# A feed-forward layer in blocks on one core: a written order of products over two pairs, a tile of its own for the first product, and later loads of residual rows

## The chip, the core and the metric

The kernel runs on one core of a Trainium2 chip. The metric is the device time of one execution in microseconds; lower is better. A core has engines with an instruction stream each: PE (matmuls), DVE (elementwise work and multiply-adds), ACT (activations, copies, casts), POOL (here a few copies, and DMA issues) and SP (DMA issues). Streams run in their own order and wait for one another through semaphores. Sums of matmuls stand in PSUM banks (here 128 x 512), everything else in SBUF tiles.

## The reference

One decoder layer over 1024 positions and a width of 1024. Ahead of what matters here lie a norm, an input projection, a convolution branch and a state-space branch, gates and a second norm. Then comes the part in which the change stands:

```python
def conv_ffn(h, w_up, dw_w, dw_b, w_down):
    u = causal_dwconv(h @ w_up, dw_w, dw_b)        # w_up 1024 x 5632, 3 taps
    gate, val = jnp.split(u, 2, axis=-1)           # 2816 columns each
    return (jax.nn.silu(gate) * val) @ w_down      # 2816 x 1024

h = layer_norm(DN_ALPHA * h + conv_ffn(h), ln2_g, ln2_b)
```

All is float32.

## The kernel before

A float32 matmul is made of three: each operand is split into a rounded part and the rest (a cast on ACT, then a subtraction on DVE), and PE adds hi x hi, hi x lo and lo x hi (lines 166 to 168). The weights so split have two halves, w[:, 0] and w[:, 1].

**up.** The 5632 columns of w_up are 44 blocks of 128, taken as 22 pairs j; a pair has a gate block (ug) and a value block (uv), each 128 channels by 1024 positions, in an early and a late half of 512. Both blocks of a pair and both halves of positions come from seven products in place of eight, of four chunks of 128 in the inner dimension and three matmuls each, so 12 matmuls by 512 columns. The sums of the hidden rows which they need (b11, b21, b22, t1, t2, t3, t4) are made once ahead of it, those of the weights for each pair by up_weights: four additions on DVE over the loaded blocks ra and rb, and casts and subtractions into w_ue (for b11 and b21), w_s24 (for t2 and b22), w_s10 (t1 and t4) and w_s3 (t3).

For the first LEAD = 8 pairs the products b11 and b21 are made in advance (up_first) and lie in DRAM as first_scr; here these are called the lead pairs, with five products each (60 matmuls) in the main loop. The other 14 have all seven (84).

In up_rest, ps is a bank that holds b11; ACT copies it to s; PE adds t2 to the same bank, ACT copies that to s again; then t1 is added and copied to uv's late half, then b22 and copied to ug's late half. Each of these four steps waits for the copy of the one ahead of it, since PE goes on adding in the bank that ACT reads. The other bank, pz, holds t3 and then t3 + t4; DVE subtracts from both. py holds b21, which DVE adds to s for ug's early half. For a lead pair b11 is not computed: both halves of first_scr[j] are loaded into ug, and ACT copies the late half of it into ps (line 878) before PE adds to it. There are three u tiles; a pair takes two, in turn.

Behind the products, each block has a causal convolution with three taps (one step on ACT, line 894, and two on DVE, line 898), then silu on ACT, the product with the gate on DVE (line 909), and a store to DRAM (b11_scr, b2_scr) for down; every second pair combines its block with that of an earlier pair in four additions and stores t32_scr and t41_scr.

**down.** Seven products again, now each over 11 steps k of 12 matmuls; load(p, k) brings an activation block (dr from b11_scr, b2_scr, t32_scr or t41_scr) and weight blocks of w_down (c, do), casts and subtracts them into w_dn. load_rows brings the rows of the residual stream from DRAM into the tile rows, four halves of rows a call, on POOL's queue. Its calls stand at k == 4 of products 0, 1, 2 and 4.

**Order.** A scheduler orders each engine's instructions from the program's order and priorities: a block under tc.high_priority moves ahead by the number given. Pools with a number of buffers per tag hold back the writer of a tile until the last reader of its slot is done; the w tiles (tag w) have few slots, s has two, raw (rb) three. The helper that does the cast is split_pair (lines 740 and 741); product makes the matmuls; bank(i) takes a PSUM bank from one of two sets, shown as acc and sm.

Of the kernel before, what the change touches and what calls it, by code (L numbers as in the profile page):

```python
# [8 lines left out]
F32 = mybir.dt.float32  # L9
F32R = mybir.dt.float32r  # L10
AF = mybir.ActivationFunctionType
ALU = mybir.AluOpType
# [4 lines left out]
P = 128  # L17
D = 1024
T = 1024
# [37 lines left out]
def kernel(  # L57
# [35 lines left out]
    ident = const.tile([P, P], F32, name="ident")  # L93
    make_identity(nc, ident)
    state_stack = ExitStack()
    statep = state_stack.enter_context(pool("states", side="right"))
# [5 lines left out]
    V.memset(ones, 1.0)  # L102
    mean_w = const.tile([P, P], F32, name="mean_w")
    V.memset(mean_w, 1.0 / D)
    eps = const.tile([P, 1], F32, name="eps")
# [17 lines left out]
    V.tensor_scalar_mul(kind_neg, kind[:, 0:2], -1.0)  # L123
    pc = const.tile([P, PC_N + 80], F32, name="pc")
    a_log = statep.tile([P, HEADS], F32, name="a_log")
# [108 lines left out]
    def ln_in(hh):  # L234
        hT = big_tile(f"hT{hh}")
        with pool(f"lnin{hh}", side="right") as pl:
# [12 lines left out]
            if first:  # L249
                SY.dma_start(pc[:, :PC_N], pcol)  # L250
                SY.dma_start(a_log, prow[RW_AL : RW_AL + HEADS].partition_broadcast(P))
                SY.dma_start(dskip, prow[RW_SD : RW_SD + HEADS].partition_broadcast(P))
# [562 lines left out]
    def up_first(upp, fp, bl, j):  # L815

        if j < LEAD - 1:
            t = weights(wup[2 * j], f"ue{j}")
            w = [t[:, i, :] for i in range(2)]
        else:  # L820
            with tc.high_priority(offset=4000):
                st = wst.tile([P, D], F32, tag="st", name=f"st_ue{j}")
                SY.dma_start(st, wup[2 * j])
                w = [upp.tile([P, D], F32R, tag="o", bufs=3, name=f"ue{i}_{j}") for i in range(2)]
                A.copy(w[0], st)
                V.tensor_tensor(out=w[1], in0=st, in1=w[0].bitcast(F32), op=ALU.subtract)
        ps = bank(1)
        for q, block in enumerate(("b11", "b21")):
            product(ps, lambda i: w[i][:, q * HALF : (q + 1) * HALF], bl[block], q == 0)
            f = fp.tile([P, HALF], F32, tag="first", bufs=2, name=f"first{q}_{j}")  # L830
            A.copy(f, ps)
            A.dma_start(first_scr[j][1 - q], f)

# [22 lines left out]

    def up_rest(upp, us, bl, j, before, ws):

# [3 lines left out]
        ug, uv = us[2 * j % 3], us[(2 * j + 1) % 3]  # L862
        s = upp.tile([P, HALF], F32, tag="s", bufs=2, name=f"s{j}")
        early, late = slice(2, 2 + HALF), slice(2 + HALF, 2 + T)
        ps, pz = bank(1), bank(0)
        if ue:
            product(ps, lambda i: ue[:, i, :HALF], bl["b11"], True)
            A.copy(s, ps)
            py = bank(1)
            product(py, lambda i: ue[:, i, HALF:], bl["b21"], True)  # L870
            V.tensor_tensor(out=ug[:, early], in0=s, in1=py, op=ALU.add)
        else:
            with tc.high_priority(offset=2500):
                SY.dma_start(
                    ug[:, 2 : 2 + T].rearrange("p (q n) -> p q n", q=2),
                    first_scr[j].rearrange("q p n -> p q n"),
                )
            A.copy(ps, ug[:, late])
        product(ps, lambda i: w24[:, i, :HALF], bl["t2"], False)
        A.copy(s, ps)  # L880
        product(pz, lambda i: w3[:, i], bl["t3"], True)
        product(ps, lambda i: w10[:, i, :HALF], bl["t1"], False)
        A.copy(uv[:, late], ps)
        V.tensor_tensor(out=uv[:, late], in0=pz, in1=uv[:, late], op=ALU.subtract)
        product(pz, lambda i: w10[:, i, HALF:], bl["t4"], False)
        V.tensor_tensor(out=uv[:, early], in0=pz, in1=s, op=ALU.subtract)
        product(ps, lambda i: w24[:, i, HALF:], bl["b22"], False)
        A.copy(ug[:, late], ps)
        os = []
# [28 lines left out]
        if j < NK:  # L918
            G.dma_start(b11_scr[j], ov[:, early])
            return ov  # L920
        SY.dma_start(b2_scr[j - NK], ov)
        a, b, t = before, ov, og
        V.tensor_tensor(out=t[:, early], in0=a[:, late], in1=b[:, late], op=ALU.subtract)
# [6 lines left out]
    def down(upp, dp):  # L930
# [18 lines left out]

        def load_rows(p):  # L950
            t0, cs = {0: (0, E), 1: (0, L), 2: (4, L), 4: (4, E)}[p]
            for t in range(t0, t0 + 4):
                G.dma_start(rs[t][:, cs], h1_scr[t * P : (t + 1) * P, cs])
# [137 lines left out]
        for p, (banks, first, then) in enumerate(products):  # L1091
            end = NK - LAST if p == 6 else NK
            for k in range(end):
# [3 lines left out]
                if k == 4 and p in (0, 1, 2, 4):  # L1097
                    load_rows(p)
            ws = {k: load(p, k) for k in range(end, NK)}
# [24 lines left out]
    state_stack.close()  # L1124
    mixT = combine(1, hT, yT)
    ffn_stack = ExitStack()
    qp = ffn_stack.enter_context(pool("ffq", side="right"))
# [6 lines left out]
    with pool("firsts", side="right") as fp:  # L1134
        for j in range(LEAD):
            if j == LEAD - 1:
                ws = up_weights(upp, 0)
            up_first(upp, fp, bl, j)
    before = None
    for j in range(NF):  # L1140
        before, ws = up_rest(upp, us, bl, j, before, ws), None
    ffn_stack.close()
# [101 lines left out]
```

## Time and profile before

| | us |
|---|---|
| median of three runs | 2029.7 |
| lowest and highest | 2026.96, 2030.37 |
| the profiled execution | 2030.47 |
| its span in the trace | 2028.8 |
| PE busy in the span | 1975.8 (97%) |
| DVE busy | 1695.8 (84%) |
| ACT busy | 1017.4 (50%) |
| POOL busy | 175.5 (9%) |

In the profile L166 is a line of the kernel; a row of a group has the line, the engine, the operation, the tile written and the tiles read, the count, then busy time, mean ns of one, and the idle time of the engine ahead of them with what ended it. A row of the waits has who waits for whom, the total in us, the number of times and the longest. In rows in order of time the first two numbers are start and length. The mean granted clock of PE is 0.995 of full speed. up's main loop runs from about 1391 to 1800, and down from there to the end.

### The profile page before, as it was taken

How to read it: one execution, taken by the hardware profiler on the slowest of the kernel's cores; microseconds unless marked ns; L12 is line 12 of the kernel's file. 1: busy time of each engine (PE TensorE's matmuls, PEld its weight loads, DVE VectorE, ACT ScalarE, POOL GpSimd, SP SyncE). 2: the span in 40 equal slices, each digit the busy share in tenths (PEclk: the TensorE clock that was granted, in tenths of full speed). 3: DMA queues.
4: the chain of work that ended last, by engine and by line, in shares of the span. 5: the costliest groups of instructions: out<-in, count | busy, mean ns of one | idle time of the engine just before them, and what ended most of it. 6: DMA issues, size and time to landing. Idle time of an engine off the chain costs nothing.

```text
span 2028.8 us, 24542 instructions
## 1 busy us (share of the span) xinstructions
PE 1975.8 (97%) x9164; PEld 1622.4 (80%) x9164; DVE 1695.8 (84%) x2261; ACT 1017.4 (50%) x1480; POOL 175.5 (9%) x140
## 2 busy tenths in 40 slices
PE   7999999999999999999999999999999999999998
PEld 6888888888788888888888888887777777777886
DVE  7599999989766869999998976596897777788768
ACT  4465654556453356665454645364554534443432
POOL 2010101001400000110100130010000000030000
PEclk9999999999999999999999999999999999999999
DMA  6222233333546522222323354565342222367563
GB/s 219 94 64 93 79 103 104 99 104 101 175 131 220 194 94 73 91 81 77 126 89 104 109 167 139 186 234 202 135 172 83 99 107 102 101 252 252 176 225 109
DMA packets 96903, 272.20 MB, mean 134 GB/s; under 512 B 11088, under 2 KB 11088, under 8 KB 96784
## 3 DMA queue, kind: packets, MB, share of 16 engines
q1 hardware_dynamic: 88864, 246.78, 36.8%
q0 software_dynamic: 5616, 19.66, 2.5%
q10 hardware_dynamic: 2304, 4.20, 0.6%
q8 instruction: 72, 1.18, 0.2%
q14 instruction: 47, 0.39, 0.1%
HBM read 221.05 MB, written 49.55 MB: 133 GB/s over the span
## 4 chain that ended last, share of the span: by engine, by line
PE 72%; DVE 19%; DMA 4%; issue 3%; ACT 2%; SPq 0%; DVEq 0%; ACTq 0%
PE acc L166 19%; PE acc L167 19%; PE acc L168 19%; DVE c L420 6%; PE sm L168 3%; PE sm L166 3%; PE sm L167 3%; PE sm L534 2%; PE acc L357 1%; DVE xbc L375 1%; DVE fo L898 1%; DMA dr<-b_scr 1%; PE sm L515 1%; PE sm L192 1%; PE sm L523 1%
## 5 line engine op out<-in xcount | busy, mean ns | idle before, releaser
L420 DVE SCALAR_TENSOR_TENSOR c<-v,pc,c 128x512 f32<-128x512 f32 x480 | 374.9, 804 | 6.3 <-ACT c L409 4.9
L478 POOL TENSOR_TENSOR au<-seg_mv,head_of 128x1024 fp32r<-128x1024 f32 x32 | 76.4, 2388 | 959.1 <-PE sm L487 728.8
L166 PE MATMUL acc<-hT,w_c 128*128 128x512 f32 x352 | 141.0, 401 | 0.0
L167 PE MATMUL acc<-hT,w_c 128*128 128x512 f32 x352 | 140.6, 399 | 0.0
L168 PE MATMUL acc<-hT,w_c 128*128 128x512 f32 x352 | 138.4, 393 | 0.0
L898 DVE SCALAR_TENSOR_TENSOR fo<-u,pc,fo 128x1024 f32<-128x1024 f32 x88 | 111.4, 1279 | 7.5 <-ACT fo L894 7.4
L375 DVE SCALAR_TENSOR_TENSOR xbc<-u,pc,xbc 128x512 f32<-128x512 f32 x144 | 109.9, 775 | 0.7 <-ACT xbc L373 0.5
L166 PE MATMUL acc<-h1s,w_s 128*128 128x512 f32 x264 | 103.6, 396 | 6.3 <-ACT s L880 3.7
L167 PE MATMUL acc<-h1s,w_s 128*128 128x512 f32 x264 | 102.9, 390 | 0.0
L168 PE MATMUL acc<-h1s,w_s 128*128 128x512 f32 x264 | 102.8, 391 | 0.0
L167 PE MATMUL acc<-w_z,hT 128*128 128x512 f32 x256 | 100.8, 394 | 0.0
L166 PE MATMUL acc<-w_z,hT 128*128 128x512 f32 x256 | 100.8, 401 | 0.0
L168 PE MATMUL acc<-w_z,hT 128*128 128x512 f32 x256 | 100.7, 396 | 0.0
L1032 ACT CAST w_dn<-dr 128x1024 fp32r<-128x1024 f32 (+1 forms) x73 | 60.9, 842 | 75.8 <-DVE dr L962 37.8
L154 ACT CAST w_c<-st_c 128x1024 fp32r<-128x1024 f32 x50 | 52.5, 1051 | 88.9 <-PE acc L168 68.2
L1033 DVE TENSOR_TENSOR w_dn<-dr,w_dn 128x1024 fp32r<-128x1024 f32 (+1 forms) x73 | 69.8, 963 | 15.3 <-ACT w_dn L1032 15.1
L167 PEld LDWEIGHTS acc<-hT,w_c 128*128 128x128 f32 x352 | 66.1, 188 | 16.9 <-issue 3.9
L168 PEld LDWEIGHTS acc<-hT,w_c 128*128 128x128 f32 x352 | 66.1, 188 | 16.2 <-issue 2.6
L166 PEld LDWEIGHTS acc<-hT,w_c 128*128 128x128 f32 x352 | 66.1, 188 | 15.9 <-issue 2.6
L166 PE MATMUL acc<-h1b,w_ue 128*128 128x512 f32 x168 | 67.3, 400 | 11.1 <-ACT w_ue L740 8.4
L155 DVE TENSOR_TENSOR w_c<-st_c,w_c 128x1024 fp32r<-128x1024 f32 x47 | 60.5, 1288 | 20.2 <-ACT w_c L154 20.2
L740 ACT CAST w_s<-rb 128x1024 fp32r<-128x1024 f32 x22 | 23.0, 1048 | 98.4 <-PE sm L168 63.8
(353 smaller groups left out, 5755.4 us busy)
## 6 DMA issues: line engine op xcount, KB each, us to landing
st_c<-wcol SPq DMA_DIRECT2D x50, 512.0 KB, 3.5
st_z<-wz SPq DMA_DIRECT2D x32, 512.0 KB, 3.5
st_wo<-wo SPq DMA_DIRECT2D x24, 512.0 KB, 4.0
ra<-wup SPq DMA_DIRECT2D x22, 512.0 KB, 3.6
rb<-wup SPq DMA_DIRECT2D x22, 512.0 KB, 3.4
t_scr<-fo POOLq DMA_DIRECT2D x22, 512.0 KB, 3.8
dr<-t_scr SPq DMA_DIRECT2D x44, 256.0 KB, 3.5
dr<-wdown SPq DMA_DIRECT2D x38, 256.0 KB, 3.9
```

Of the source, the lines that this page charges most:

```text
L154: A.copy(w[:, 0, :], st)
L155: (eng or V).tensor_tensor(out=w[:, 1, :], in0=st, in1=w[:, 0, :].bitcast(F32), op=ALU.subtract)
L166: TE.matmul(ps, wa(0), xa(0), start=start, stop=False, skip_group_check=more)
L167: TE.matmul(ps, wa(0), xa(1), start=False, stop=False, skip_group_check=more)
L168: TE.matmul(ps, wa(1), xa(0), start=False, stop=stop, skip_group_check=more)
L375: V.scalar_tensor_tensor(out=o, in0=u[:, k : k + HALF], scalar=pc[:, wc + k : wc + k + 1], in1=o, op0=ALU.mult, op1=ALU.add,)
L420: V.scalar_tensor_tensor(out=accs[i], in0=v[:, k : k + HALF], scalar=pc[:, wc + k : wc + k + 1], in1=accs[i], op0=ALU.mult, op1=ALU.add,)
L478: G.tensor_tensor(out=au, in0=seg_mv[:, c, :].unsqueeze(1).to_broadcast([P, 8, P]), in1=head_of[:, g, :].unsqueeze(2).to_broadcast([P, 8, P]),
L534: TE.matmul(py[:, hs], m[:, h, :], xs[:, hs], start=True, stop=True)
L898: V.scalar_tensor_tensor(out=o, in0=u[:, k : k + T], scalar=pc[:, wc + k : wc + k + 1], in1=o, op0=ALU.mult, op1=ALU.add,)
L1032: A.copy(w[:, 0, cs], src)
L1033: V.tensor_tensor(out=w[:, 1, cs], in0=src, in1=w[:, 0, cs].bitcast(F32), op=ALU.subtract)
```

## The change

**Pairs.** up_rest becomes a generator, up_pair, that stops twice. Its three pieces are: b11 (or the load of it) with its copy, and for a lead pair t2; b21 and t2 (where the pair has them), t3 and t1; b22, t4 and all that follows. The loop calls the pieces of pairs j and j - 1 in turn, under tc.manual_schedule for PE, which keeps PE's instructions in the order in which they are written. For a pair with seven products PE then has b11(j+1), b22(j), t4(j), b21(j+1), t2(j+1), t3(j+1), t1(j+1); in the lead t2(j+1), b22(j), t4(j), t3(j+1), t1(j+1). The copies of s, of ps and of uv's late half, and the DVE steps behind them, get a high priority of 300.

**First products.** For a lead pair the half that goes into ps is loaded into s, which has three slots now, and the other half straight into ug's early half; before, one transfer brought both into ug. The halves of first_scr change places for it (b11 is at index 0).

**Row loads.** load_rows takes the weight tile w of step k and, ahead of its loads, copies 4 numbers of it per partition into the first columns of the row halves to be loaded, on POOL. The loads overwrite them, so they wait for the copy, and the copy for the cast of w. All the values copied are overwritten.

**Room.** The tile mean_w has a pool of its own, closed ahead of up; pc loses 80 columns of padding that were not used.

The core of the diff:

```diff
-    mean_w = const.tile([P, P], F32, name="mean_w")
-    V.memset(mean_w, 1.0 / D)
+    mean_stack = ExitStack()
+    mean_w = mean_stack.enter_context(pool("mean", side="right")).tile([P, P], F32, name="mean_w")
+    V.memset(mean_w, 1.0 / D)
...
-    pc = const.tile([P, PC_N + 80], F32, name="pc")
+    pc = const.tile([P, PC_N], F32, name="pc")
...
-            A.dma_start(first_scr[j][1 - q], f)
+            A.dma_start(first_scr[j][q], f)
...
-    def up_rest(upp, us, bl, j, before, ws):
+    def up_pair(upp, us, bl, j, kept, ws):
...
-        s = upp.tile([P, HALF], F32, tag="s", bufs=2, name=f"s{j}")
+        s = upp.tile([P, HALF], F32, tag="s", bufs=3, name=f"s{j}")
         early, late = slice(2, 2 + HALF), slice(2 + HALF, 2 + T)
         ps, pz = bank(1), bank(0)
+
+        def t2():
+            product(ps, lambda i: w24[:, i, :HALF], bl["t2"], False)
+            with tc.high_priority(offset=300):
+                A.copy(s, ps)
+
         if ue:
             product(ps, lambda i: ue[:, i, :HALF], bl["b11"], True)
-            A.copy(s, ps)
+            with tc.high_priority(offset=300):
+                A.copy(s, ps)
+        else:
+            with tc.high_priority(offset=2500):
+                SY.dma_start(s, first_scr[j][0])
+            with tc.high_priority(offset=300):
+                A.copy(ps, s)
+            SY.dma_start(ug[:, early], first_scr[j][1])
+            t2()
+        yield
+        if ue:
             py = bank(1)
             product(py, lambda i: ue[:, i, HALF:], bl["b21"], True)
-            V.tensor_tensor(out=ug[:, early], in0=s, in1=py, op=ALU.add)
-        else:
-            with tc.high_priority(offset=2500):
-                SY.dma_start(
-                    ug[:, 2 : 2 + T].rearrange("p (q n) -> p q n", q=2),
-                    first_scr[j].rearrange("q p n -> p q n"),
-                )
-            A.copy(ps, ug[:, late])
-        product(ps, lambda i: w24[:, i, :HALF], bl["t2"], False)
-        A.copy(s, ps)
+            with tc.high_priority(offset=300):
+                V.tensor_tensor(out=ug[:, early], in0=s, in1=py, op=ALU.add)
+            t2()
         product(pz, lambda i: w3[:, i], bl["t3"], True)
         product(ps, lambda i: w10[:, i, :HALF], bl["t1"], False)
-        A.copy(uv[:, late], ps)
-        V.tensor_tensor(out=uv[:, late], in0=pz, in1=uv[:, late], op=ALU.subtract)
+        with tc.high_priority(offset=300):
+            A.copy(uv[:, late], ps)
+            V.tensor_tensor(out=uv[:, late], in0=pz, in1=uv[:, late], op=ALU.subtract)
+        yield
+        product(ps, lambda i: w24[:, i, HALF:], bl["b22"], False)
+        A.copy(ug[:, late], ps)
         product(pz, lambda i: w10[:, i, HALF:], bl["t4"], False)
         V.tensor_tensor(out=uv[:, early], in0=pz, in1=s, op=ALU.subtract)
-        product(ps, lambda i: w24[:, i, HALF:], bl["b22"], False)
-        A.copy(ug[:, late], ps)
...
-        def load_rows(p):
+        def load_rows(p, w):
             t0, cs = {0: (0, E), 1: (0, L), 2: (4, L), 4: (4, E)}[p]
+            G.tensor_copy(
+                rows.rearrange("p (t n) -> p t n", n=D)[:, t0 : t0 + 4, cs.start : cs.start + 1],
+                w[:, 0, :4].bitcast(F32).unsqueeze(2),
+            )
             for t in range(t0, t0 + 4):
                 G.dma_start(rs[t][:, cs], h1_scr[t * P : (t + 1) * P, cs])
...
-    before = None
-    for j in range(NF):
-        before, ws = up_rest(upp, us, bl, j, before, ws), None
+    kept = []
+    with tc.manual_schedule(engines={mybir.EngineType.PE}):
+        pairs = [up_pair(upp, us, bl, 0, kept, ws)]
+        next(pairs[0])
+        next(pairs[0])
+        for j in range(1, NF + 1):
+            if j < NF:
+                pairs.append(up_pair(upp, us, bl, j, kept, None))
+                next(pairs[j])
+            next(pairs[j - 1], None)
+            if j < NF:
+                next(pairs[j])
```

**Rows moved on ACT in the lead.** ACT's rows of before around the start of lead pair 4; the copy of acc517 from u2 is the copy of the loaded half into ps:

```order
L883 COPY u1_10909<-acc515_11529 128x512
L878 COPY acc517_11634<-u2_10910 128x512
L740 CAST w_s10_4_11627<-rb4_11617 128x1024
L888 COPY u0_10908<-acc515_11529 128x512
L894 ACTIVATE fo12_11598<-u0_10908,pc_107 128x1024
L740 CAST w_s24_5_11723<-ra5_11714 128x1024
L894 ACTIVATE fo34_11602<-u1_10909,pc_107 128x1024
L880 COPY s4_11633<-acc517_11634 128x512
```

The same place now (acc517 is again the bank of pair 4, acc519 that of pair 5):

```order
L741 CAST w_s3_6_11803<-s3_6_11792 128x512
L881 COPY acc521_11807<-s6_11806 128x512
L920 ACTIVATE fo12_11645<-fo12_11645,pc_110 128x1024
L894 COPY u0_10912<-acc517_11601 128x512
L871 COPY s5_11706<-acc519_11707 128x512
L741 CAST w_s10_5_11700<-rb5_11690 128x1024
L898 COPY u2_10914<-acc517_11601 128x512
L741 CAST w_s24_6_11797<-ra6_11788 128x1024
```

The copy into the bank reads s in place of u and stands one pair further ahead; the copy of s for pair 5 stands two rows ahead of that of u for pair 4 (from acc517).

**Rows moved on PE and ACT among the pairs with seven products.** PE of before, where pair 16 begins:

```order
L167 MATMUL sm544_12826<-h1b2_10852,w_s10_14_12818 128x512
L168 MATMUL sm544_12826<-h1b2_10852,w_s10_14_12818 128x512
L168 MATMUL acc543_12825<-h1s1_10448,w_s24_14_12815 128x512
L167 MATMUL acc546_12952<-h1s3_10450,w_s24_15_12942 128x512
L168 MATMUL acc546_12952<-h1s3_10450,w_s24_15_12942 128x512
L166 MATMUL acc549_13085<-h1b1_10382,w_ue16_13067 128x512
L167 MATMUL acc549_13085<-h1b1_10382,w_ue16_13067 128x512
L166 MATMUL acc551_13100<-h1b1_10382,w_ue16_13067 128x512
```

Here t4 of pair 14 (sm544) ends, then come the last matmuls of b22 of pair 14 and t2 of pair 15, and b11 and b21 of pair 16 follow at once. PE now, at the start of b11 of pair 16:

```order
L167 MATMUL acc546_12929<-h1s2_10453,w_s10_15_12922 128x512
L168 MATMUL acc546_12929<-h1s2_10453,w_s10_15_12922 128x512
L169 MATMUL acc546_12929<-h1s2_10453,w_s10_15_12922 128x512
L167 MATMUL acc549_13056<-h1b1_10386,w_ue16_13038 128x512
L168 MATMUL acc549_13056<-h1b1_10386,w_ue16_13038 128x512
```

It follows t1 of pair 15 and has its product to itself; ahead of t1 stand t3, t2 and, four products back, b21 of pair 15, the last reader of w_ue15. On ACT the casts for pair 16 were, before,

```order
L740 CAST w_s24_15_12942<-ra15_12930 128x1024
L883 COPY u2_10910<-acc543_12825 128x512
L740 CAST w_s10_15_12945<-rb15_12932 128x1024
L740 CAST w_ue16_13067<-ra16_13063 128x1024
L888 COPY u1_10909<-acc543_12825 128x512
L880 COPY s15_12951<-acc546_12952 128x512
```

and are now

```order
L741 CAST w_s24_15_12919<-ra15_12907 128x1024
L898 COPY u1_10913<-acc543_12796 128x512
L906 ACTIVATE fo7_12970<-u1_10913,pc_110 128x1024
L741 CAST w_s10_15_12922<-rb15_12909 128x1024
L906 ACTIVATE fo29_12974<-u2_10914,pc_110 128x1024
L741 CAST w_ue16_13038<-ra16_13034 128x1024
```

The cast of w_ue16 stood right behind that of w_s10 of pair 15, with the copies of u and s behind both; now two steps of the convolution stand between the casts, and the copy of u ahead of them.

**Rows moved on POOL.** Its last DMA issues and copies before, where down begins:

```order
L993 COPY c3_13855<-dr_5_13952 128x512
L919 DMA b11_scr10_144<-fo32_13703 128x512
L953 DMA rows_13856<-h1_scr_125 128x512 x16
L927 DMA t32_scr10_166<-fo21_13826 128x1024
L928 DMA t41_scr10_177<-fo32_13703 128x1024
L957 DMA ln2_g_14450<-prow 128x1024
L957 DMA ln2_b_14452<-prow 128x1024
```

and now:

```order
L1010 COPY c3_13870<-dr_5_13967 128x512
L931 DMA b11_scr10_147<-fo32_13754 128x512
L965 COPY rows_13871<-w_dn0_4_13971 128x4
L970 DMA rows_13871<-h1_scr_128 128x512 x4
L940 DMA t32_scr10_169<-fo21_13840 128x1024
L941 DMA t41_scr10_180<-fo32_13754 128x1024
L974 DMA ln2_g_14468<-prow 128x1024
L974 DMA ln2_b_14470<-prow 128x1024
L965 COPY rows_13871<-w_dn1_4_14198 128x4
L970 DMA rows_13871<-h1_scr_128 128x512 x4
L965 COPY rows_13871<-w_dn2_4_14448 128x4
L970 DMA rows_13871<-h1_scr_128 128x512 x4
```

The sixteen row loads were one group, ahead of the last two stores of up (t32_scr10, t41_scr10); now four of them stand there behind a copy from w_dn of product 0, step 4, and the other twelve behind copies from w_dn of products 1, 2 and 4.

More of the change, by code (lines that the diff above doesn't have):

```diff
@@ L249, in ln_in @@
             if first:
-                SY.dma_start(pc[:, :PC_N], pcol)
+                SY.dma_start(pc, pcol)
                 SY.dma_start(a_log, prow[RW_AL : RW_AL + HEADS].partition_broadcast(P))
@@ L919, in up_rest @@
             G.dma_start(b11_scr[j], ov[:, early])
-            return ov
+            kept.append(ov)
+            return
         SY.dma_start(b2_scr[j - NK], ov)
-        a, b, t = before, ov, og
+        a, b, t = kept.pop(), ov, og
         V.tensor_tensor(out=t[:, early], in0=a[:, late], in1=b[:, late], op=ALU.subtract)
@@ L1097, in down @@
                 if k == 4 and p in (0, 1, 2, 4):
-                    load_rows(p)
+                    load_rows(p, w)
             ws = {k: load(p, k) for k in range(end, NK)}
@@ L1125 @@
     mixT = combine(1, hT, yT)
+    mean_stack.close()
     ffn_stack = ExitStack()
```

## The prediction

> **What bounds the kernel now.** I began with the profile's busy times and its lines of the chain that ended last, then narrowed to the end of the program, where the diff acts.
>
> ```profile
> span 2028.8 us, 24542 instructions
> PE 72%; DVE 19%; DMA 4%; issue 3%; ACT 2%; SPq 0%; DVEq 0%; ACTq 0%
> ```
>
> PE carries 72% of the chain. The number of matmuls does not change, so only time in which PE stands still can be won. All waits of PE from the first of the pairs that up_rest makes to the middle of down's first product:
>
> ```profile
> PE acc L166 <- ACT w_ue L740: 8.4, 6, 1.4
> PE acc L166 <- ACT s L880: 3.7, 5, 0.9
> PE acc L166 <- ACT w_dn L1032: 3.4, 1, 3.4
> PE acc L166 <- ACT u L883: 2.7, 3, 1.7
> PE sm L166 <- ACT w_s L740: 2.0, 3, 1.3
> PE acc L167 <- DVE w_dn L1033: 0.2, 1, 0.2
> ```
>
> The columns are the engine and line that waits, whom it waits for, total us, times, longest. Together 20.4 us in 19 waits, nearly all for a copy or a cast on ACT, an engine that is busy half of the time. How these lengths turn into lost time is read off PE's rows in order of time:
>
> ```profile
> 1821.81 0.39 PE L167 MATMUL acc<-w_dn 128*128 128x512 f32 x1
> ...
> 1824.76 0.39 PE L168 MATMUL acc<-w_dn 128*128 128x512 f32 x1
> 1828.52 0.80 PE L166 MATMUL acc<-w_dn 128*128 128x512 f32 x1 [3.38 <-ACT w_dn L1032]
> 1829.12 0.63 PE L167 MATMUL acc<-w_dn 128*128 128x512 f32 x1
> ...
> 1834.24 0.47 PE L167 MATMUL acc<-w_dn 128*128 128x512 f32 x1
> 1834.54 0.40 PE L168 MATMUL acc<-w_dn 128*128 128x512 f32 x1
> ```
>
> From the first to the third row are 13 steps in 2.95 us: a matmul starts every 0.227 us, though its record is 0.39 long. So a wait costs its printed length plus 0.16 us, and a product of 12 matmuls takes 2.73 us. Here 3.76 us pass between two starts: 3.53 lost. Behind it the matmuls come every 0.43 us until 1834.24: 13 starts in 5.72 us where 2.96 would do, another 2.76. PE's idle time here costs **6.3 us** in all.
>
> The stretches differ in what fills them:
>
> ```profile
> 1440.00:1480.00 40.00, 34.34 (x144) 26.13 (x143) 34.45 (x40) 18.78 (x25) 1.61 (x3) 1.00 0.39 141
> 1480.00:1520.00 40.00, 38.32 (x165) 30.36 (x164) 35.11 (x41) 21.86 (x27) 2.67 (x5) 1.00 0.54 190
> 1560.00:1600.00 40.00, 38.60 (x170) 31.40 (x168) 31.37 (x37) 18.08 (x23) 1.60 (x3) 1.00 0.28 99
> 1790.00:1830.00 40.00, 35.65 (x151) 28.17 (x150) 28.28 (x32) 20.29 (x29) 10.89 (x18) 0.97 0.81 302
> 1850.00:1950.00 100.00, 100.00 (x443) 82.80 (x442) 80.55 (x112) 39.92 (x53) 0.00 (x0) 1.00 0.67 208
> ```
>
> Columns: window, length, busy PE, PEld, DVE, ACT, POOL, granted clock, DMA share, GB/s. In the eight lead pairs (1400 to 1518) DVE is busy 69.6 of 80 us; in the pairs with seven products 31.4 of 40; at down's beginning the DMA engines carry 302 GB/s; behind 1850 PE never stops.
>
> **The change, part by part.**
>
> *Pairs with seven products.* Six waits for the cast of w_ue, one per two pairs: 8.4 + 6 x 0.16 = 9.4 us. Their cause on ACT:
>
> ```profile
> 1597.08 1.05 ACT L740 CAST w_s<-rb 128x1024 fp32r<-128x1024 f32 x1 [9.72 <-PE sm L168]
> 1598.04 1.04 ACT L740 CAST w_ue<-ra 128x1024 fp32r<-128x1024 f32 x1
> 1598.98 0.58 ACT L888 COPY u<-acc 128x512 f32<-128x512 f32 x1
> 1599.46 0.59 ACT L880 COPY s<-acc 128x512 f32<-128x512 f32 x1
> ```
>
> The cast of w_ue stands behind a cast of w_s whose slot comes free only with the end of t4, and in PE's order the first product that needs w_ue follows t4 after three matmuls: 0.7 us of cover for two casts of 1.0 us. In the new order the slot for w_ue comes free with b21, and t2, t3 and t1 stand between: 3 x 2.73 = 8.2 us of cover for a cast of 1.04 and a subtraction of 1.2 (row of L741 below). All six go: **-9.4 us**. What is late next is the copy of s from t2. Its s is still read by the DVE addition behind b21, and in DVE's new order that addition stands behind a chain begun by the end of t4. With the durations of these rows,
>
> ```profile
> L898 DVE SCALAR_TENSOR_TENSOR fo<-u,pc,fo 128x1024 f32<-128x1024 f32 x26 | 32.8, 1279 | 0.9 <-ACT fo L894 0.9
> L741 DVE TENSOR_TENSOR w_s<-rb,w_s 128x1024 fp32r<-128x1024 f32 x7 | 8.6, 1224 | 10.3 <-ACT w_s L740 10.3
> L886 DVE TENSOR_TENSOR u<-sm,s 128x512 f32<-128x512 f32 x7 | 4.8, 688 | 6.2 <-PE sm L168 6.2
> ```
>
> it is: subtraction from t4 0.69, a convolution step 1.28, subtraction of w_s10 1.22, two more steps 2.56, the addition 0.69, and the copy 0.59: 7.0 us. PE comes to t1 three products behind t4, at 8.2 us. The slack is **1.2 us**, if DVE is not behind when t4 ends. With DVE at 78% of the window's time I take no stall.
>
> *Lead pairs.* The waits for s, u and w_s above belong to them, but for one each of s and u that stand at the end of up:
>
> ```profile
> PE acc L166 <- ACT s L880: 0.7, 1, 0.7
> PE acc L166 <- ACT u L883: 0.2, 1, 0.2
> ```
>
> That leaves 3.0 + 2.5 + 2.0 in nine waits, with 9 x 0.16 lost 8.9 us. ACT itself stands for the load that brings both first products into u:
>
> ```profile
> ACT acc L878 <- DMA u<-first_scr: 20.1, 5, 4.5
> ...
> 1434.62 0.59 ACT L878 COPY acc<-u 128x512 f32<-128x512 f32 x1 [4.33 <-DMA u<-first_scr]
> 1435.23 1.05 ACT L740 CAST w_s<-rb 128x1024 fp32r<-128x1024 f32 x1
> ```
>
> That load must wait until a u is free, and the casts of w_s stand behind the copy. The new s tile (three of them) is loaded without a u, so these 20.1 us of ACT go. Between a product and the reader of its copy there is now another product, 2.73 us for a copy of 0.59. But in the new order the copy of s for pair j+1 stands ahead of the copy of u for pair j in every second pair; following ACT's rows by these durations I find two waits of some 1.3 us left, at b22 of pairs 3 and 5. And DVE has little room: 69.6 of 80 us is 87%, and 118 us of lead shortened by 8.9 would make it 94%. Bounds: nothing won (DVE sets the pace) to 8.9. I take 8.9 - 2.6: **-6.3 us**, nearer to the end that the named waits give, since DVE's share stays under 100%.
>
> *First of the pairs.* Ahead of them PE waits for the copies of first:
>
> ```profile
> 1388.35 0.39 PE L167 MATMUL sm<-h1b,w_s 128*128 128x512 f32 x1
> 1391.46 0.79 PE L166 MATMUL acc<-h1b,w_ue 128*128 128x512 f32 x1 [2.73 <-ACT first L831]
> ```
>
> What stands ahead is unchanged, so the wait stays; but the two matmuls of t3 that fill it now come later: 2 x 0.23, **+0.5 us**.
>
> *Between up and down.* The two waits just quoted, 0.7 + 0.2 + 2 x 0.16, go by the same order: **-1.2 us**. The 0.2 for w_dn stays.
>
> *Row loads.* ACT's row ahead of the 3.38 us, and the issues from 1790 to 1850:
>
> ```profile
> 1827.85 0.62 ACT L1032 CAST w_dn<-dr 128x512 fp32r<-128x512 f32 x1 [7.30 <-DMA dr<-b_scr]
> rows<-h_scr POOLq DMA_DIRECT2D x16, 256.0 KB, 8.2
> c<-wdown SPq DMA_DIRECT2D x10, 256.0 KB, 7.4
> ```
>
> The cast waits 7.3 us for a transfer that shares 302 GB/s with sixteen row loads. Twelve of these now wait for the casts of later products: 12 x 0.262 MB = 3.15 MB, 10.4 us at 302 GB/s. A third of it is enough for the 3.53 us, and with the wait its slow matmuls go: **-6.3 us**; bounds 0 (the transfers are in another order than I think) and -6.3. The twelve loads fall behind 1850 in three lumps of 1.05 MB, 3.5 us each at that rate; at worst each delays a weight by its whole length, 10.5 us. I take 0: 208 GB/s leave room, and PE had no wait there. The four copies on POOL are not in the trace; the nearest row is of 128x512,
>
> ```profile
> L993 POOL COPY c<-dr 128x512 f32<-128x512 f32 x5 | 6.3, 1290 | 19.5 <-PE acc L168 12.3 <-DMA dr<-wdown 7.2
> ```
>
> so 0 to 4 x 1.3 us beside everything else. Queued behind the first of them on POOL are the last two stores of up (t32, t41), the next row loads and those for the last norm, nothing that PE reads within the next product. I take 0. The moved mean_w and the 80 columns less of pc move no work: 0.
>
> The Trainium skill, page "TensorE: Matmul & The Clock Gate", section "What's actually happening", says that the half clock comes after an idle window of about 3.4 us, free-running, and lifts after about as long busy. The rows above show it behind idle 3.38 us, but for 5.7 us. With 3.4 us instead the slow part would cost an estimated 1.7 in place of 2.76 and the sum would lose 1.1 us; the row decides.
>
> **Sum**, on the profiled execution of 2030.47 us (span 2028.8 and 1.7 around it): -9.4 - 6.3 + 0.5 - 1.2 - 6.3 = -22.7, 2007.8. The median of the three runs is 0.8 lower: **2007 us**.
>
> **Rivals.**
> - *DVE sets the lead's pace.* For it: 87% busy now. Against: its waits there are for ACT. The 6.3 is not won: 2013.
> - *The wait in down stays*, because the transfer is late for its place in SP's queue (ten c loads of 7.4 us stand around it). Against: the row loads alone are 3.15 MB. 6.3 not won: 2013; with the one above 2020.
> - *The lead is won whole*, no wait at b22: 2.6 more, 2004.5; and if the wait at 1391 also shrinks, some us more.
> - *Slower: s is late in each pair.* If DVE is behind by more than the 1.2 us when t4 ends, PE waits at t1 in each of the 14 pairs with seven products. Behind by 2.8 us it takes 14 x 1.6 = 22.4, all of the gain; by two steps and a w_s subtraction (3.8 us), 14 x 2.6 = 36: 2044. For it: the addition is last of a chain of seven rows, and the old order let the scheduler put other matmuls there. Against: DVE is idle 8.6 of 40 us.
> - *It doesn't do what it says.* The row loads are seen behind the copies in POOL's order and the products are in the written order on PE, so little speaks for this; with partly the same waits, within 4 us of before.
>
> **How the numbers follow.** Forecast 0.56, with the lead won whole 0.12; DVE's pace or down's wait, one or both, 0.17; not doing what it says 0.06; slower by s 0.09. The range takes the forecast, the whole lead with up to 3 us beyond it, and both terms lost: 2001 to 2020, leaving 2 in 10 out with the edges of these cases. A measurement of this kernel tells about 0.2% (4 us) from no change. Faster 0.85, within 0.2% 0.06, slower 0.09.
>
> **What would show it.** Right: no row of PE waiting for w_ue; PE busy throughout 1550 to 1750; ACT not waiting for first_scr; rows issues spread over down; clock 1.00 around 1825. Wrong: PE rows waiting for s or u in the pairs (DVE late), DVE above 95% in the lead, a w_dn wait with a dr load behind it, or waits behind 1850. I am wrong altogether if waits in the new order are rare but over 2.7 us, since each would bring 2.8 us of half clock with it.

## The result, and the profile after

| | before | changed |
|---|---|---|
| median of four runs, us | 2028.5 | 2006.8 |
| lowest to highest | 2026.96 to 2030.37 | 2005.08 to 2008.13 |
| profiled execution | 2030.47 | 2007.04 |
| its span | 2028.8 | 2005.2 |

The ratio of the times is 0.9892, with a 95% interval of 0.9875 to 0.9909: 22 us faster, against 23 predicted. The time came out where it was forecast, but not every term of the sum did: one that was put at nothing cost 5.6 us, and one that was put at 0.5 us more came out at 4.1 us less.

All waits of PE in the changed kernel from 1380, ahead of the pairs, to the end of down (waiter, whom for: total us, times, longest):

```profile
PE acc L167 <- ACT u L894: 2.3, 2, 1.2
PE acc L167 <- ACT first L832: 1.3, 2, 0.8
```

Four waits are left. There is none for w_ue, s, w_s or w_dn. The stretches of the changed kernel, with the same columns as before:

```profile
1440.00:1480.00 40.00, 38.84 (x168) 31.22 (x167) 38.55 (x46) 22.28 (x27) 2.68 (x5) 1.00 0.56 197
1480.00:1520.00 40.00, 38.84 (x168) 31.30 (x167) 36.00 (x40) 23.02 (x27) 2.15 (x4) 1.00 0.35 119
1560.00:1600.00 40.00, 40.00 (x176) 32.57 (x175) 32.45 (x39) 19.39 (x24) 1.61 (x3) 1.00 0.29 104
1850.00:1950.00 100.00, 100.00 (x439) 82.01 (x438) 75.65 (x98) 41.83 (x53) 3.35 (x7) 1.00 0.68 221
```

PE is without a pause among the seven-product pairs, and DVE is busy 38.6 of 40 us in the first half of these 80 us and 36.0 in the second. The last row holds a surprise: PE is busy all of the 100 us, as before, but begins 439 matmuls there where before it began 443.

The first matmul on w_ue starts between 1349.8 and 1354.5 us in the profiled executions of this case. What moves it was not looked into, so from here on the runs are compared by the time from the first matmul on w_ue to the last of the program. Its two ends in PE's rows in order of time, first before, then changed:

```profile
1350.34 0.39 PE L166 MATMUL acc<-h1b,w_ue 128*128 128x512 f32 x1
...
2018.87 0.39 PE L168 MATMUL acc<-last 128*128 128x512 f32 x1
```

```profile
1351.57 0.39 PE L167 MATMUL acc<-h1b,w_ue 128*128 128x512 f32 x1
...
1995.57 0.39 PE L169 MATMUL acc<-last 128*128 128x512 f32 x1
```

668.5 us before and 644.0 changed: 24.5 less. To divide this, take the steps, the times from one matmul's start to the next. Most are between 0.22 and 0.24 us; the longer ones are the pauses, the slow matmuls at half clock, and a step or two behind each pause, as here in before:

```profile
1597.34 0.39 PE L168 MATMUL acc<-h1s,w_s 128*128 128x512 f32 x1
1599.13 0.50 PE L166 MATMUL acc<-h1b,w_ue 128*128 128x512 f32 x1 [1.40 <-ACT w_ue L740]
1599.47 0.39 PE L167 MATMUL acc<-h1b,w_ue 128*128 128x512 f32 x1
1599.70 0.40 PE L166 MATMUL acc<-h1b,w_ue 128*128 128x512 f32 x1
```

The step of 1.79 us holds the wait, and the one behind it is 0.34. All that steps over 0.27 us have above 0.2275 adds up to 35.25 us before and 5.15 changed, 30.1 less. The missing 5.6 us are in the usual steps between one matmul and the next.

### The profile page after: what moved, and what is told of

Read it like the earlier page. It is cut to its first block, busy times and chain, and to the rows that moved or that the text cites. A ratio compares the mean times of both kernels' runs of the same rounds, so it can differ in the third digit from the quotient of the medians.

```text
span 2005.2 us, 24594 instructions
## 1 busy us (share of the span) xinstructions
PE 1971.1 (98%) x9164; PEld 1620.4 (81%) x9164; DVE 1693.9 (84%) x2261; ACT 1022.5 (51%) x1480; POOL 178.0 (9%) x144
## 5 line engine op out<-in xcount | busy, mean ns | idle before, releaser
L167 PE MATMUL sm<-h1b,w_s 128*128 128x512 f32 x176 | 69.6, 396 | 0.0
L169 PE MATMUL sm<-h1b,w_s 128*128 128x512 f32 x176 | 69.3, 394 | 0.0
```

The lines of the kernel that those rows point to most:

```text
L167: TE.matmul(ps, wa(0), xa(0), start=start, stop=False, skip_group_check=more)
L169: TE.matmul(ps, wa(1), xa(0), start=False, stop=stop, skip_group_check=more)
```

## The experiments

"End" in this table is that time from the first matmul on w_ue to the last matmul, in each profiled execution. Ratios are against before on the same chip; where there is none, the kernel was run once.

| kernel | end, us | ratio (95%) |
|---|---|---|
| before | 668.5 | 1 |
| changed | 644.0 | 0.9892 (0.9875 to 0.9909) |
| changed, 80 columns back | 637.1 | 0.9864 (0.9846 to 0.9883) |
| changed, 24 columns | 644.6 | 0.9901 (0.9877 to 0.9925) |
| changed, 48 columns | 642.4 | |
| changed, t3 behind t2 | 645.4 | 0.9903 (0.9887 to 0.9919) |
| both: 80 columns, t3 behind t2 | 641.2 | 0.9879 (0.9864 to 0.9895) |
| changed, row loads not held | 645.5 | 0.9905 (0.9888 to 0.9922) |
| before, row loads held | 658.8 | 0.9974 (0.9963 to 0.9984) |
| changed, without the s tile | 694.7 | |
| changed, PE ordered by the scheduler | 645.6 | 0.9893 (0.9877 to 0.9910) |
| the same, 80 columns back | 643.4 | 0.9869 (0.9852 to 0.9885) |
| before, with the s tile | 654.7 | 0.9935 (0.9921 to 0.9950) |
| changed, one addition doubled | 664.8 | |

### The 80 columns behind pc

```diff
-    pc = const.tile([P, PC_N], F32, name="pc")
+    pc = const.tile([P, PC_N + 80], F32, name="pc")
```

> The changed kernel with the 80 columns behind pc put back; every instruction stands in the same order on every engine, only what lies behind pc in SBUF moves by 320 bytes. The trace of the change shows a start of a matmul every 0.2289 us in down (1850 to 1950) where before had 0.2267, and 0.2303 among the seven-product pairs where before had 0.2295; over some 900 and 1450 matmuls that is 2.0 and 1.2 us, the 3.2 us by which the sum of the waits gone exceeds the time gained. Theory A, the place of the tiles sets the spacing: 0.2267 and 0.2295 come back, and the profiled span is 3 us shorter than that of the change. Theory B, the spacing comes from something else in the change (the copies and loads of rows on POOL during down, the closer work of the other engines): 0.2289 and 0.2303 stay, the span is the same within 1 us.

Same instructions in the same order on every engine, and the end is 6.9 us shorter, the profiled span 1999.4 us. Rows of the windows from 1560 and from 1850, first changed, then with the 80 columns:

```profile
1560.00:1660.00 100.00, 100.00 (x436) 81.48 (x435) 82.33 (x97) 47.91 (x58) 4.29 (x8) 1.00 0.30 108
```

```profile
1560.00:1660.00 100.00, 100.00 (x440) 82.34 (x439) 83.30 (x99) 47.86 (x57) 4.83 (x9) 1.00 0.29 106
1850.00:1950.00 100.00, 100.00 (x443) 82.80 (x442) 74.03 (x95) 43.71 (x57) 2.35 (x5) 1.00 0.64 213
```

Down has its 443 matmuls per 100 us again, a start every 0.2267 us and not 0.2289. Among the pairs it is 0.2280, against 0.2303 in the change. In before it is 0.2284 there without the longer steps behind the waits; the 0.2295 of the expectation holds them. So theory A holds, with twice the gain that it forecast: it started from the 0.2295, and left out the lead pairs, which gain 1.6 us. By the steps over 0.27 us this kernel waits 0.6 us less than the change (one wait of 0.4 us for first is gone); the other 6.3 us are the spacing. Its median of 2000.3 us is below before's on the same chip (2026.5), and below those of the two variants of the change without the 80 columns that ran beside it (2007.5 with row loads not held, 2008.2 with t3 behind t2).

Which address matters? Two more sizes:

> The changed kernel with 24 columns (96 bytes) behind pc, the same order of instructions on every engine. The first big tile begins at byte 19712 of a partition: a multiple of 128. In the change it begins at 19616 (remainder 32 by 128, 160 by 512), with 80 columns at 19936 and in before at 20448 (remainder 96 by 128, 480 by 512). Theory A, the remainder by 128 decides, and 0 is as good as 96 or better: 0.2267 us between starts in down and 0.228 or less among the pairs, about 2000. Rival, the remainder by 512 decides (here 256) or single tiles matter: 0.2289 in down, about 2007, or between.

> The changed kernel with 48 columns (192 bytes) behind pc: the first big tile at 19808, remainder 96 by 128 as with 80 columns, but 96 by 256 and 352 by 512 (224 and 480 with 80 columns). If the remainder by 128 decides: 0.2267 us between starts in down, 0.228 among the pairs, a span near 1999.5. If that by 256 or 512 does: not those values, a span near 2005.

With 24 columns a matmul starts every 0.2294 us in down, with 48 every 0.2275 (438 and 441 per 100 us):

```profile
1850.00:1950.00 100.00, 100.00 (x438) 81.81 (x437) 77.29 (x101) 41.52 (x53) 4.51 (x9) 1.00 0.66 224
```

```profile
1850.00:1950.00 100.00, 100.00 (x441) 82.66 (x440) 76.75 (x100) 41.62 (x54) 4.35 (x8) 1.00 0.67 224
```

Among the pairs neither gains anything: 0.2309 and 0.2306, as in the change. A remainder of 0 by 128 is the worst of the four in down, and two kernels with the remainder 96 differ, so the remainder by 128 does not decide. Before and the kernel with 80 columns, both at 0.2267, have 480 by 512. In the program, the matmul operands h1s and half of the w_dn tiles lie in pools at the other end of SBUF, which did not move and have 480 too. Whether it matters that both ends agree, or that each lies at 480, wasn't tried.

### t3 behind t2 in the lead

```diff
             t2()
+            product(pz, lambda i: w3[:, i], bl["t3"], True)
         yield
         if ue:
             ...
             t2()
-        product(pz, lambda i: w3[:, i], bl["t3"], True)
+            product(pz, lambda i: w3[:, i], bl["t3"], True)
```

> The changed kernel, but for a lead pair t3 is issued right behind t2, so that t2 and t3 of pair j+1 stand between t1 of pair j and b22 of pair j. The two waits left in the lead (1.33 us each between two starts, 2.3 by the waits' list) are for a copy of u that comes after DVE has freed u. Theory A, too little cover: with 5.5 us in place of 2.7 both go, 2.3 to 2.7 us less, no new wait. Rival, DVE sets the pace in the lead (it is busy 38.6 of 40 us from 1440 to 1480): the waits move to other places, the gain is under 1 us.

The two waits went, and one came at the end of the lead. PE of this kernel, and ACT there:

```profile
1507.12 0.39 PE L169 MATMUL acc<-h1b,w_ue 128*128 128x512 f32 x1
1509.84 0.51 PE L167 MATMUL acc<-h1s,w_s 128*128 128x512 f32 x1 [2.33 <-ACT u L895]
1510.18 0.42 PE L168 MATMUL acc<-h1s,w_s 128*128 128x512 f32 x1
1510.42 0.61 PE L169 MATMUL acc<-h1s,w_s 128*128 128x512 f32 x1
1510.83 0.63 PE L167 MATMUL acc<-h1s,w_s 128*128 128x512 f32 x1
```

```profile
1509.20 0.59 ACT L895 COPY u<-acc 128x512 f32<-128x512 f32 x1 [1.07 <-DVE fo L911]
```

ACT's copy into u waits for a convolution step on DVE, and 2.33 us of PE's idle time bring half clock from 1510.4 to 1513.8. The rival holds: DVE sets the pace in the lead, so the 2.7 us were collected into one pause that costs 2.5, and another 1.6 in slow matmuls. With the 80 columns as well,

> Both edits, the 80 columns and t3 behind t2. If both first theories hold, 5 to 6 us less than the change, a median of about 2001; if only one, about 2004; if neither, 2007.

2003.2 us: only the first theory, and the edit again costs 4.1 us at the end (641.2 against 637.1), half clock included.

### The row loads

Undone in the changed kernel, and put alone into before:

```diff
-            G.tensor_copy(
-                rows.rearrange("p (t n) -> p t n", n=D)[:, t0 : t0 + 4, cs.start : cs.start + 1],
-                w[:, 0, :4].bitcast(F32).unsqueeze(2),
-            )
```

> The changed kernel without the copies ahead of the row loads, so that nothing holds the sixteen row loads back. Theory A, the loads are what made dr late in down: a wait of PE for a cast of w_dn near the tenth step of the first product comes back, up to 3.5 us, and if it is over 2.7 us half clock behind it: 3 to 7 us more than the change. Rival, the wait came from the pairs (their last stores and the c loads were late because ACT and PE were late there) and the written order alone took it away: no wait, no difference beyond 1 us.

> The kernel of before with one part of the change alone: the copy of 4 columns ahead of each group of row loads, so that twelve of the sixteen come later. Theory A, the loads alone make the wait of 3.38 us and the half clock behind it in down: both go, 6 us less than before, a median of about 2021 to 2022, and all other waits of before stay. Rival, from the run without those copies, where the loads still delayed dr by some 8 us but PE waited only 1.6: part of the wait comes from what stands ahead on SP and ACT in the old order, so a wait of 0.5 to 2 us stays: 4 to 5 us less.

ACT in the changed kernel without the copies, ahead of the cast that PE needs, and the wait of PE:

```profile
1805.54 0.62 ACT L1045 CAST w_dn<-dr 128x512 fp32r<-128x512 f32 x1 [7.80 <-DMA dr<-b_scr]
```

```profile
1806.21 0.50 PE L167 MATMUL acc<-w_dn 128*128 128x512 f32 x1 [1.61 <-ACT w_dn L1045]
```

The sixteen loads again make ACT stand 7.8 us for a dr, as in before (7.3), but PE loses 1.8 us, not 3.5, and keeps its clock. In before, holding the loads takes the whole wait away. Its waits of PE from 1780 on are now

```profile
PE acc L166 <- ACT s L880: 0.4, 1, 0.4
PE acc L166 <- ACT u L883: 0.2, 1, 0.2
PE acc L167 <- DVE w_dn L1037: 0.2, 1, 0.2
```

so theory A is right there, by the end 9.7 us, of which 6.3 are down's. The rest is the start: its wait was 2.42 us in this execution and brought no half clock. It lies some 400 us ahead of the row loads, so it is not their doing. By the medians (2028.3 to 2022.6) the gain is 5.7. So holding the loads is worth 6 us in the old order and between 1 and 2 in the new one. What else makes the difference was not tried apart. One thing that differs on SP is up's last store but one (of fo to b2_scr9): it is issued at 1758.4 us, ahead of the c loads, and in before at 1784.8, behind six of them.

### What took the waits of the pairs away

The s tile taken out of the changed kernel, the written order taken out, and the s tile alone put into before (with mean_w moved, for room):

```diff
-                SY.dma_start(s, first_scr[j][0])
+                SY.dma_start(ug[:, 2 : 2 + T].rearrange("p (q n) -> p q n", q=2), first_scr[j].rearrange("q p n -> p q n"))
...
-                A.copy(ps, s)
-            SY.dma_start(ug[:, early], first_scr[j][1])
+                A.copy(ps, ug[:, late])
```

> The changed kernel with the first products of the lead pairs loaded as before, both halves into u in one transfer, and the copy into the bank from u; the written order stays. Theory A, the written order needs the s tile: t2 of pair j+1 now stands ahead of b22 of pair j, and waits for a load that cannot start before a u is free, so PE waits 2 to 4 us in most of seven lead pairs, 15 to 30 us more than the change with half clock behind the long ones. Rival, the order alone took the waits away: no difference in the lead. The same run shows the start: the loads into u can be issued at 1381 again, 5 us ahead of where the loads into s were, so if they are what delayed the stores of first, PE's wait near 1390 is 2.7 us again and not 0.8, with half clock behind it.

```diff
-    with tc.manual_schedule(engines={mybir.EngineType.PE}):
+    if True:
```

> The changed kernel without the order written by hand for PE: the scheduler orders PE too, with the pieces in the same program order, the same priorities, tiles and row loads. Theory A, the written order took the waits for w_ue away: the scheduler again runs b11 and b21 of a pair right behind few matmuls of others, and waits for w_ue, u or s of 5 to 15 us come back among the pairs. Rival, the s tile, the priorities and the program order did it: within 2 us of the change.

> The kernel of before with one part of the change alone: the s tile with three slots into which the first products of the lead pairs are loaded (and, for its room, mean_w in a pool of its own; the 80 columns stay). No pieces of two pairs, no written order, no priorities, no row copies. Theory A, the s tile alone takes ACT's stand of 20.1 us away and the lead's waits with it, and, by holding back its own loads at the start, the wait of 2.7 us and the half clock near 1391: 9 to 13 us less than before; the six waits for w_ue (9.4 us) and the 6.3 us in down stay; a median of about 2015 to 2019. Rival, the lead's waits come from the order of the five products, each right behind the copy that it needs: 4 us less at most, those of the start.

> The changed kernel with the 80 columns back and without the order written by hand for PE. Theory A, with both in place the written order adds nothing to what the pieces in program order and the priorities give the scheduler: within 1.5 us of the same kernel with the written order (2000.3). Rival, at the closer spacing of the matmuls (0.2280 among the pairs) whole products one after the other are worth more than interleaved ones: 2 to 4 us more than that.

Without the s tile, the written order makes the lead far worse. PE's waits from 1380 to 1560:

```profile
PE acc L167 <- ACT acc L884: 36.3, 6, 6.3
PE acc L167 <- ACT first L832: 2.2, 1, 2.2
```

Six waits of 6 us, each with half clock behind it, 51 us more by the end: theory A, and longer waits than it forecast. An order that is fixed by hand has nothing to put into a wait. The second row is the start: with the loads into u issued early again the wait of PE there is 2.2 us with half clock, in the changed kernel 0.8.

Without the written order the waits hardly come back. From 1380 to 1840, PE ordered by the scheduler:

```profile
PE acc L167 <- ACT u L894: 1.6, 2, 1.1
PE acc L167 <- ACT w_ue L741: 1.4, 2, 0.7
PE acc L169 <- DVE w_s L742: 0.7, 1, 0.7
PE acc L167 <- ACT first L832: 0.2, 1, 0.2
```

3.9 us in six waits, 1.6 us more by the end: the rival holds. By the ratios (0.9893 and 0.9892) there is no difference. With the 80 columns, where the written order's kernel ends at 637.1, the scheduler's ends at 643.4, 6.3 more in this pair of executions: one wait for u of 2.2 us at the end of up with half clock behind it, two for w_ue, and shorter ones; the usual steps are alike (0.2282 and 0.2281 us among the pairs). But its profile is of the slowest of its four runs (2003.6 to 2009.5), and its ratio equals that of the other (0.9869 and 0.9864), taken in another set of runs, in which before had 2031.5 and not 2026.5. What the written order is worth at this placement, nothing or some us, stays open.

The s tile alone in before is worth 13 us by the medians (2031.5 to 2018.6), as theory A forecast, but from other places: it had the lead's waits go, and those for w_ue and the one in down stay. In the lead 5.7 us of waits stay, with half clock behind one of them, and what is left of w_ue are three waits:

```profile
PE acc L167 <- ACT u L882: 5.7, 5, 2.1
```

```profile
PE acc L167 <- ACT w_ue L741: 1.9, 3, 0.6
```

The first row is from the window 1380 to 1516, the second from 1516 to 1830, where nothing is left of down's wait but 0.2 us, though the row loads are not held, and 3.9 us of waits for u and s stand at the end of up. So the s tile, with the order that the scheduler then makes, takes two thirds of the loss in the pairs with seven products (10.5 us to 3.4, by the steps over 0.27 us) and next to nothing in the lead (10.0 to 9.5). With the pieces and their priorities as well, the lead loses 2.9 us in the written order and 2.1 in the scheduler's. Whether it is the third slot for s or the loads into it, and whether the pieces or the priorities, was not tried apart. Down's wait can be taken away in more than one place.

### One addition doubled

```diff
                 V.tensor_tensor(out=ug[:, early], in0=s, in1=py, op=ALU.add)
+                V.tensor_tensor(out=ug[:, early], in0=s, in1=py, op=ALU.add)
```

> The changed kernel with the addition of s and b21 on DVE done twice in each of the 14 pairs with seven products (the second gives the same values). The second stands behind a subtraction of w_ue (1.14 us) and a convolution step (1.19), so s is free 2.9 us later. The trace of the change has 1.40 us between the end of the copy of s and the start of t1. Theory A, this slack is the point from which the change loses: PE waits 1.5 to 1.7 us at t1 of each pair, 21 to 24 us in all, the whole gain (about 2029). Rival, the slack is wider, since PE's work queued ahead gives way: under 5 us.

```profile
PE acc L167 <- ACT s L871: 16.6, 13, 1.4
```

The row is of PE from 1516 to 1800. Thirteen waits of up to 1.4 us, 1.53 between starts, 20.8 us by the end and 2028.5 us in one run: theory A. The rival that ends on the slower side was real, and lay 1.4 us away.

## Why the prediction was right, step by step

| step | predicted | by the traces | what shows it |
|---|---|---|---|
| seven-product pairs | -9.4 | -10.5 | 10.5 before, none now |
| lead pairs | -6.3 | -7.1 | 10.0 before, 2.9 now |
| start of the pairs | +0.5 | -4.1 | 6.0 before, 1.8 now |
| between up and down | -1.2 | -2.0 | 2.0 before, none now |
| down's first product | -6.3 | -6.4 | 6.7 before, 0.3 now |
| moved tiles | 0 | +5.6 | the usual steps |
| sum | -22.7 | -24.5 | |

The traces' column counts what steps over 0.27 us have above 0.2275. The first two rows, and the fourth, are larger than predicted in the main because the prediction priced a wait at its length plus 0.16 us; with the longer step behind it a wait costs some 0.1 us more, 2 us over the waits of these rows. The fourth also holds the wait of 0.2 us for w_dn that was to stay.

**Lead.** The two waits left, at b22 of pairs 3 and 5, are where the order and the durations put them, at 1.2 us each. DVE was busy 74.6 of the 80 us, 93% where 94 was forecast, and 96% in the first half, past the 95% that the prediction named as a sign against it; the run with t3 behind t2 shows that this order of products doesn't win the rest. That "these 20.1 us of ACT go" was too much. From 1400 to 1516 ACT still has

```profile
ACT acc L881 <- DMA s<-first_scr: 5.5, 5, 1.8
```

Of 20.1 us, 5.5 are left, now for the loads into s, but none of PE's four waits is for that copy.

**Seven-product pairs.** All six waits went, and the slack that was worked out as 1.2 us was 1.40. ACT's copy of s and the first matmul of t1 in the changed kernel:

```profile
1599.58 0.59 ACT L871 COPY s<-acc 128x512 f32<-128x512 f32 x1 [0.69 <-DVE u L889]
```

```profile
1601.57 0.40 PE L167 MATMUL acc<-h1s,w_s 128*128 128x512 f32 x1
```

It ends at 1600.17, and PE comes 1.40 us later. What the step had wrong is the credit: "in the new order the slot for w_ue comes free with b21, and t2, t3 and t1 stand between" names a sufficient cause, but the scheduler, given the same tiles and pieces, leaves 1.4 of the 8.4 us, and the s tile alone, in the old program, 1.9.

**Down.** "A third of it is enough" is what before with held loads shows: without them in the way the wait is gone. But they are not the whole cause. With the s tile alone the wait went too, though the loads were not held, and in the changed kernel without the hold 1.8 of the 6.3 us are left. So most of what the prediction credits to the row loads here was won twice over.

**The start, mis-sized.** "What stands ahead is unchanged, so the wait stays" failed: what stands ahead on PE is unchanged, not on SP. SP's issues, in before,

```profile
1381.40 0.94 SPq L874 DMA_DIRECT2D u<-first_scr  x2
```

and changed:

```profile
1386.64 1.28 SPq L879 DMA_DIRECT2D s<-first_scr  x3
```

In before these two loads of 512 KB ran beside the stores of first that ACT, and behind it PE, wait for. The loads into s wait for DVE's last use of a tile that had s's place before (line 795), and with them everything behind on SP:

```profile
SPq L879 <- DVE ts L795: 4.0, 1, 4.0
```

So the stores land by 1387.3 and not 1390.8. The wait fell from 2.73 to 0.84 and 0.42 us, and the clock stayed up. Two runs bear this out: with the loads into u again the wait is 2.2 us, and with the s tile alone in before it is 0.2. Not all of the 4.1 us is sure to be won in each execution: in before with held row loads nearly the same wait, 2.42 us, brought no half clock, and its start lost 3 us less than that of before.

**Moved tiles, mis-sized.** "The moved mean_w and the 80 columns less of pc move no work: 0" is true of work, but the wider steps cost 5.6 us against before, and 6.3 against the same kernel with the 80 columns. This miss and the opposite ones, 4.6 us at the start and 2.8 in the other rows, nearly cancel, and that is luck. The step that left it out is "only time in which PE stands still can be won": the time between two matmuls of a busy PE changes too. With the 80 columns back the median is 2000.3 us, just below the range of 2001 to 2020; without the gain at the start it would have been near 2011.

**Half clock.** The trace of before agreed with the Trainium skill (page "TensorE: Matmul & The Clock Gate", section "What's actually happening") that idle PE brings half clock; the return took 5.7 us there, longer than the about 3.4 us of that section. In the run with t3 behind t2 the slow stretch lasts 3.4 us. So both lengths occur. The prediction feared half clock only for waits over 2.7 us. Pauses down to 2.13 us brought it, which is also less than the idle window of about 3.4 us that it quotes.

## What to carry to other kernels

Before crediting a new order, give the scheduler the new buffers and the same pieces: here the order by hand added 1.6 us of 24 in one pair of executions, and nothing by the ratios, where nothing else differed (what it adds with the 80 columns is open), and without the buffer that it needs it cost 51. A tile that is moved or a padding that is dropped belongs in the sum even if no instruction changes: compare the time between two matmuls in a stretch without waits (443 and 439 per 100 us). And a wait at one place can depend on loads that another change delays, so look at what each new tile's first load waits for and what is queued behind it.

## What the runs showed of the hardware

- The time from one 512-column matmul to the next depends on where the tiles lie: 0.2267, 0.2275, 0.2289 and 0.2294 us in the same code of down, where the first byte of the tiles moved has the remainders 480, 352, 160 and 256 by 512. The cause wasn't found.
- Half clock does not follow from the length of a pause alone: 2.42 us brought none (before with held row loads), while 2.33 us (t3 behind t2), 2.20 us (changed, without the s tile) and 2.13 us (before with the s tile) did. In that last kernel a pause of 1.99 us brought none, and behind the 2.13 us it set in only with the fifth matmul:

```profile
1464.46 0.50 PE L167 MATMUL acc<-h1s,w_s 128*128 128x512 f32 x1 [2.13 <-ACT u L882]
1464.80 0.39 PE L168 MATMUL acc<-h1s,w_s 128*128 128x512 f32 x1
1465.03 0.39 PE L169 MATMUL acc<-h1s,w_s 128*128 128x512 f32 x1
1465.26 0.40 PE L167 MATMUL acc<-h1s,w_s 128*128 128x512 f32 x1
1465.50 0.51 PE L168 MATMUL acc<-h1s,w_s 128*128 128x512 f32 x1
1465.81 0.63 PE L169 MATMUL acc<-h1s,w_s 128*128 128x512 f32 x1
1466.23 0.63 PE L167 MATMUL acc<-h1s,w_s 128*128 128x512 f32 x1
```
